# A minimum and a small product take their second operand as a scalar, and the attention stage is planned anew

## The chip, the cores and the metric

The kernel runs on one core of one Trainium2 chip. The metric is the device time of one launch in microseconds; the time before is a median of three runs. The engines are called TensorE (PE in the rows, PEld its weight loads), VectorE (DVE), ScalarE (ACT), GpSimd (POOL) and SyncE (SP, which issues the transfers).

## The reference, cut to what matters

One layer of a diffusion backbone: a normalised, modulated input projection feeds two groups of attention heads, then come an output projection and a SwiGLU feed-forward part. The change lies in attention. 1024 latent queries read 1024 latent keys and 256 context keys in one softmax:

```python
a = jax.nn.softmax(s1, axis=-1) - lam * jax.nn.softmax(s2, axis=-1)   # 4 heads, group A
a = jax.nn.softmax(s, axis=-1)                                        # 8 heads, group B
```

In group A each head has two score maps, s1 and s2, and the weighted difference of their softmaxes multiplies the values; in group B each head has one. Each softmax needs its row's maximum over all 1280 keys.

## The kernel before, in words

**Stages.** From 0 to about 324 us the kernel projects the input and writes queries, keys and values to HBM. From 324 to about 840 us it runs attention: two units of group B, then eight units of group A (4 heads by 2 halves of the queries), then the rest of group B. After that come the output projection and the feed-forward part.

**One block.** A unit of group A is four blocks of 128 queries. For a block TensorE writes two score maps of 1280 columns into one accumulator tile S of five banks: `latent` 0 and 1 fill 1024 columns each, `context` 256 columns of both maps in the bank between them (L1056). VectorE takes the negated maximum of the context columns of both maps in one instruction, `max_context` (nmc, L1068), and of the latent columns of each map, `max_latent` (nm, L1072). `least` (L1076) takes the smaller of the two, one number per partition; it is the bias of ScalarE's exponential `exp` (L1090), which also sums its row. S exists once, so the next block's `context` waits for both exponentials of this block.

**Between the maps.** In group A `factor` (L1097 a reciprocal, L1098 a product) makes -lam times the ratio of the two row sums, one number per partition. GpSimd then multiplies the second map by it (`weigh`, L1101) and adds the first (`combine`, L1104), both over 1280 columns. In group B GpSimd only divides by the row sum (`normalise`, L1110).

**Values.** For each of the ten 128-key chunks of a unit TensorE transposes four blocks (L1118), ScalarE copies the result as the high part (`high`, ph, L1122), VectorE subtracts it for the low part (`low`, pl, L1126), and TensorE multiplies both by the values (L1135, L1140).

**Order.** `attention_graph` lists all operations of the stage with an engine, an assumed duration, dependencies and a due number; `schedule` plays them as a list scheduler (of the operations ready on an engine the lowest due number goes first), and they are issued in the order of the planned starts. The due number is the block's or chunk's position plus an entry of the table PRIO, one entry per kind of operation. Each engine works through its own list strictly in order. The planned times do not depend on what the other engines do in the same moment.

The functions that the change touches, and what calls them:

Of the kernel before, what the change touches and what calls it, by code (L numbers as in the profile page):

```python
# [13 lines left out]
ALU = mybir.AluOpType  # L14
# [69 lines left out]
                put(user)  # L84


PRIO = {'up': 11.727086, 'mod': -18.756409, 'sum_mod': -32.213338, 'TA': 4.147972, 'TB': 8.034109, 'lagA': 0.698127, 'lagB': 0.960591, 'near': 0.126904, 'Alatent0': -26.812639, 'Acontext': -21.646222, 'Alatent1': 2.987414, 'Amax_latent0': -4.873014, 'Amax_context': -26.762829, 'Amax_latent1': -2.132328, 'Aexp0': -31.715337, 'Aexp1': 12.171988, 'Atranspose': 4.62933, 'Ahigh': 11.648332, 'Alow': 37.646643, 'Asum': 9.444701, 'Blatent0': 3.505773, 'Bcontext': 4.634551, 'Blatent1': 7.767885, 'Bmax_latent0': 2.818406, 'Bmax_context': -34.678605, 'Bmax_latent1': 7.503355, 'Bexp0': 30.917087, 'Bexp1': 13.50608, 'Btranspose': 0.882797, 'Bhigh': -25.097498, 'Blow': -2.25778, 'Bsum': 4.842969, 'factor': -19.46868, 'weigh': -21.351391, 'combine': -24.776362, 'inverse': 7.726575, 'normalise': -24.649633, 'square': 2.409828, 'diagonal': -2.156322, 'load': 0, 'out': 33.135816}


def attention_graph(prio=PRIO):  # L90

# [3 lines left out]
    def op(engine, time, deps, name, *args, kind=None, late=0.0):  # L95
        o = Op(engine, time, deps, base[0] + late + prio[kind or name], name, args)
        ops.append(o)
        return o
# [3 lines left out]
    def slot(tag, bufs):  # L102

        got = slots.setdefault(tag, [])
        return got[-bufs] if len(got) >= bufs else None

    x = [None, None]
    acc_free = None
    low_sum = []
# [4 lines left out]
    def after(tag, o):  # L114

        if tag in order:
            o.deps.append(order[tag])
        order[tag] = o
        return o

    def block(n, A):

        nonlocal x
        u, qh, b, j = n
        k = "A" if A else "B"
        w = 1.0 if A else 1.5
        need = [loads[u], loads[u, qh], loads.get((u, qh, j))]
        first = op("PE", 0.86 * w, need + [x[0]], "latent", n, 0, kind=k + "latent0")
        ctx_ = op("PE", 0.43 * w, need + x, "context", n, kind=k + "context")
        second = op("PE", 0.86 * w, need + [x[1]], "latent", n, 1, kind=k + "latent1")  # L130
        mc = op("DVE", 0.6, [ctx_], "max_context", n, kind=k + "max_context")
        m0 = op("DVE", 1.13, [first], "max_latent", n, 0, kind=k + "max_latent0")
        m1 = op("DVE", 1.13, [second], "max_latent", n, 1, kind=k + "max_latent1")
        l0 = op("DVE", 0.07, [m0, mc], "least", n, 0, kind=k + "max_latent0")
        l1 = op("DVE", 0.07, [m1, mc], "least", n, 1, kind=k + "max_latent1")
        tags = [("e1", 3) if A and b == 0 else ("e", 8), ("e2", 3) if A else ("e", 8)]
        x = []
        for i, l in enumerate((l0, l1)):
            x.append(after("exp", op("ACT", 1.3, [l, slot(*tags[i])], "exp", n, i, kind=k + f"exp{i}")))
            slots[tags[i][0]].append(None)  # L140
        for key in ((u, qh), (u, qh, j), ("kv", kvs[-1])):
            scored.setdefault(key, []).extend((first, second, ctx_))
        if A:
            f = op("DVE", 0.2, x, "factor", n)
            wt = op("Pool", 1.31, [f], "weigh", n)
            c = op("Pool", 2.84, [wt], "combine", n)
            slots["e2"][-1] = c
            return [c]
        done = []
        for i in range(2):  # L150
            f = op("DVE", 0.08, [x[i]], "inverse", n, i)
            done.append(op("Pool", 1.31, [f], "normalise", n, i))
        return done

    def chunk(c, ready, A):
        nonlocal acc_free
        k = "A" if A else "B"
        kc = c[3]
        t = after("T", op("PE", 0.436, ready + (T[-2] if len(T) > 1 else []), "transpose", c, kind=k + "transpose"))
        old = low_sum[-3:][:1] if len(low_sum) > 2 else []  # L160
        h = after("high", op("ACT", 0.478, [t] + old, "high", c, kind=k + "high"))
        l = after("low", op("DVE", 0.602, [h] + old, "low", c, kind=k + "low"))
        T.append([h, l])
        sh = op("PE", 0.43 if A else 0.215, [h, acc_free if kc == 0 else None] + low_sum[-1:], "sum_high", c, kind=k + "sum")
        low_sum.append(op("PE", 0.215, [l, sh], "sum_low", c, kind=k + "sum"))
        return t

    def finish(u, qh, j, A):
        nonlocal acc_free
        if A:  # L170
            acc_free = op("ACT", 0.478, low_sum[-1:] + low_done, "evac_a", u, qh, kind="Ahigh")
            evac[u, qh] = acc_free
        else:
            a = op("ACT", 0.478, low_sum[-1:] + (cats[-2] if j == 0 and len(cats) > 1 else []), "evac_b", u, qh, j, kind="Bhigh")
            acc_free = op("DVE", 0.602, [a], "add_b", u, qh, j, kind="Blow")
            if j == 0:
                cats.append([])
            if (u, qh) == (HA, 0):
                parked.append(((u, qh, j), acc_free))
            else:  # L180
                cat((u, qh, j), [acc_free], cats[-1])

    def cat(n, deps, to):
        h = op("ACT", 0.52, deps, "cat_high", *n, kind="Bhigh", late=5.0)
        to.extend([h, op("DVE", 0.6, [h], "cat_low", *n, kind="Blow", late=5.0)])

    cats, parked, kvs, qs, ropes = [], [], [], [], []

# [51 lines left out]
    low_done = []  # L240
    vt_last, t, root = {}, 0.0, None
    for i, (u, qh, j) in enumerate(units):
        A = u < HA
        per = prio["TA"] * 4 if A else prio["TB"] * 2
        base[0] = t
        if u != (units[i - 1][0] if i else None):
            kvs.append(i)
            old = kvs[-3:][:1] if len(kvs) > 2 else []
# [8 lines left out]
        for b in range(4 if A else 2):  # L257
            base[0] = t + b * (prio["TA"] if A else prio["TB"])
            ready += block((u, qh, b, j), A)
# [22 lines left out]
        for tag in ("e1", "e"):  # L282
            slots[tag] = [o or last for o in slots.get(tag, ())]
        vt_last[kvs[-1]] = low_sum[-1]
        finish(u, qh, j, A)
        if i == 2 * HA + 1:
            for n, o in parked:
                cat(n, [o, low_sum[-1]], cats[0])
# [7 lines left out]
    for d in range(FIRST + 1):  # L296
        f = op("DMA", 3.0, [before_last, fetched[d], summed if d > 1 else None], "fetch_out", d, kind="load")
        h = op("ACT", 0.95, [f], "high_out", d, kind="out")
# [7 lines left out]
def tile_hybrid_diffattn_mla_dit_layer(  # L306
# [18 lines left out]
    ACT, DVE, POOL, PE = nc.scalar, nc.vector, nc.gpsimd, nc.tensor  # L325
    dma = nc.sync.dma_start

    def pool(stack, name, side=None, space=None, bufs=1):
        kw = {}
        if side:  # L330
            kw["side"] = side
        if space is not None:
            kw["space"] = space
        if space is not DRAM:
            kw["reuse_waits"] = "tile"
        return stack.enter_context(tc.tile_pool(name=name, bufs=bufs, **kw))
# [35 lines left out]
    nlam = const.tile([P, 1], F32, name="nlam")  # L372
# [77 lines left out]
    x = sp.tile([P, KD, NT], F32, name="x")  # L450
# [135 lines left out]
    low = [(0, i) for i in range(3)] + [(1, i) for i in range(2)] + [(2, i) for i in range(2)]  # L586
# [121 lines left out]
    for j, (ps, (b, i)) in enumerate(zip(lows, low)):  # L708
        n = SLICES[i][1]
# [204 lines left out]
    for which, dst in ((0, KA), (1, QA)):  # L914
        for h in range(HA):
            next_weights()
            w = ahead.pop(0)
# [62 lines left out]
    class Attention:  # L980
# [92 lines left out]

        def least(self, n, i):
            nm, nmc = self.s[n][0][:, i:i + 1], self.s[n][1][:, i:i + 1]
            DVE.tensor_tensor(nm, nm, nmc, ALU.min)  # L1076

        def exp(self, n, i):
            u, qh, b, j = n
# [14 lines left out]
        def factor(self, n):  # L1094
            u, qh, b, j = n
            l1, l2 = l1st[:, u * 8 + qh * 4 + b:u * 8 + qh * 4 + b + 1], self.s[n][2][:, 1:2]
            DVE.reciprocal(l2, l2)  # L1097
            DVE.scalar_tensor_tensor(l2, l2, l1, nlam, ALU.mult, ALU.mult)  # L1098

        def weigh(self, n):  # L1100
            POOL.tensor_scalar(self.e[n, 1], self.e[n, 1], self.s[n][2][:, 1:2], 1.0, ALU.mult, ALU.mult)  # L1101
# [151 lines left out]
    ops = attention_graph()  # L1253
    schedule(ops, PRIO["near"])
    ops.sort(key=lambda o: o.start)
# [89 lines left out]
    op = pool(st, "outp", side="right")  # L1345
# [195 lines left out]
    with tc.manual_schedule(engines=ENGINES):  # L1541
        ws = [load_out(d) for d in range(KD - 2, KD)]
        for d in range(KD - 2, KD):
            ps = mm_tile()
            project(1, d, ps, ws.pop(0), range(8))
            if d == KD - 2:
                residual(1, d, ps)
                first = [Hidden(0, False), None]
# [64 lines left out]
    for j in range(2, NJ - 1):  # L1613
        h, ahead = ahead, Hidden(j + 1)
# [285 lines left out]
```

## Time and profile before

| what | value |
|---|---|
| time, median of 3 runs | 1641.59 us (1640.61 to 1644.83) |
| the profiled execution | 1640.7 us, its span 1638.9 us |
| TensorE busy over the span | 1519.1 us (93%) |
| VectorE busy | 1193.3 us (73%) |
| ScalarE busy | 759.6 us (46%) |
| GpSimd busy | 798.5 us (49%) |

Busy time is the time in which the engine has an instruction in work, including time in which an instruction that has begun is held up. Shares over the whole span hide that the stages have different limits, so the rows below go by stretches.

### The profile page before, as it was taken

Reading aid. Unit: us, or ns where it says so; the run is one execution under the profiler, and the core shown is the slowest. Engines: PE = TensorE matmul, PEld = TensorE weight load, DVE = VectorE, ACT = ScalarE, POOL = GpSimd, SP = SyncE. Lnnn points to the kernel's source line nnn. Section 1 sums busy time; section 2 is a strip of 40 time slices with the busy share of each in tenths; the row PEclk is TensorE's granted clock in tenths of the full one; section 3 lists DMA queues with packets and bytes.
Section 4 is the critical chain, followed back from the end, with each engine's and each line's share of the span. In section 5 each row is a group of like instructions: output and inputs, shape, how many; then the busy total and the mean of one; then the engine's idle time right before and its main releaser. Section 6 shows DMA issues by size and latency. Waiting matters only on the chain.

```text
span 1638.9 us, 20678 instructions
## 1 busy us (share of the span) xinstructions
PE 1519.1 (93%) x7323; PEld 1214.8 (74%) x7323; DVE 1193.3 (73%) x1642; ACT 759.6 (46%) x1192; POOL 798.5 (49%) x551
## 2 busy tenths in 40 slices
PE   4899999987778899999999989999999999999887
PEld 2577888765566678788877857888888888888766
DVE  5757565579999988999975588655555556869893
ACT  5443421265556557677764444333333333444251
POOL 2435335435656656755622275755544441437531
PEclk8999999999999999999999989999999999999997
DMA  8436987592332345453217412322222225963432
GB/s 252 138 96 223 319 280 226 186 265 87 84 90 72 71 97 142 110 157 82 65 52 212 154 45 71 110 90 84 77 84 78 77 78 185 369 235 136 159 116 103
DMA packets 153923, 227.70 MB, mean 139 GB/s; under 512 B 11215, under 2 KB 80859, under 8 KB 153819
## 3 DMA queue, kind: packets, MB, share of 16 engines
q1 hardware_dynamic: 153547, 226.11, 44.7%
q8 instruction: 58, 0.95, 0.2%
q14 instruction: 46, 0.38, 0.1%
q10 hardware_dynamic: 272, 0.26, 0.0%
HBM read 172.53 MB, written 53.81 MB: 138 GB/s over the span
## 4 chain that ended last, share of the span: by engine, by line
PE 58%; DVE 23%; DMA 6%; issue 4%; POOL 4%; ACT 3%; SPq 1%; DVEq 0%; ACTq 0%; POOLq 0%
PE mm L1427 24%; PE mm L1713 8%; PE S L1056 7%; DVE nm L1076 4%; PE T L1118 4%; DVE nm L1072 4%; PE mm L1355 3%; DVE pl L1126 3%; PE acc L1135 2%; DVE block L347 2%; PE acc L1140 2%; PE mm L410 2%; PE mm L600 1%; DVE nmc L1068 1%; PE ps L1355 1%
## 5 line engine op out<-in xcount | busy, mean ns | idle before, releaser
L1090 ACT ACTIVATE e<-S,nm 128x1280 f32<-128x1280 f32 x128 | 170.1, 1329 | 104.3 <-DVE nm L1076 79.9
L1056 PE MATMUL S<-kt,qt 128*128 128x512 f32 (+1 forms) x768 | 200.9, 370 | 13.6 <-ACT e L1090 11.4
L1713 PE MATMUL mm<-block 128*128 128x512 f32 x792 | 182.0, 392 | 6.8 <-DVE block L347 6.8
L1118 PE MATMUL T<-ident,e 128*128 128x128 f32 x960 | 147.8, 277 | 36.1 <-DVE pl L1126 32.1
L1713 PEld LDWEIGHTS mm<-block 128*128 128x128 f32 x792 | 149.5, 189 | 39.1 <-DVE block L347 8.1
L1122 ACT ACTIVATE ph<-T 128x512 fp32r<-128x512 f32 x240 | 142.1, 597 | 75.8 <-PE T L1118 71.7
L1118 PEld LDWEIGHTS T<-ident,e 128*128 128x128 f32 x960 | 115.1, 142 | 77.6 <-issue 29.9
L1126 DVE TENSOR_TENSOR pl<-T,ph 128x512 fp32r<-128x512 f32 x240 | 161.3, 682 | 15.0 <-ACT ph L1122 12.5
L1056 PEld LDWEIGHTS S<-kt,qt 128*128 128x128 f32 x768 | 132.2, 192 | 49.6 <-ACT e L1090 26.3
L1072 DVE TENSOR_REDUCE nm<-S 128x1 f32<-128x1024 f32 x128 | 155.8, 1217 | 15.6 <-PE S L1056 14.3
L1110 POOL TENSOR_SCALAR e<-e,ls 128x1280 f32<-128x1280 f32 x64 | 85.9, 1342 | 116.5 <-DVE ls L1107 101.0
L1135 PE MATMUL acc<-ph,vt 128*128 128x512 f32 x320 | 131.1, 450 | 2.0 <-ACT ph L1122 1.1
L1427 PE MATMUL mm<-fresh,wh 128*128 128x512 f32 x352 | 113.8, 402 | 3.3 <-DVE fresh L1580 2.9
L1427 PE MATMUL mm<-block,wh 128*128 128x512 f32 x352 | 112.3, 400 | 0.0
L1532 POOL TENSOR_TENSOR hd<-acc,v 128x512 f32<-128x512 f32 x22 | 29.6, 1344 | 147.3 <-DVE acc L1528 135.7
L344 ACT ACTIVATE wh<-wf 128x1024 fp32r<-128x1024 f32 (+1 forms) x51 | 52.2, 1026 | 103.6 <-issue 64.1
L1140 PE MATMUL acc<-pl,vt 128*128 128x512 f32 x240 | 99.3, 414 | 0.0
L1300 POOL TENSOR_TENSOR acc<-acc,sq 128x512 f32<-128x512 f32 x23 | 35.2, 1530 | 129.6 <-ACT sq L1298 129.0
L410 PE MATMUL mm<-hH,wh 128*128 128x512 f32 (+1 forms) x256 | 95.2, 372 | 0.0
L1104 POOL TENSOR_TENSOR e<-e,e 128x1280 f32<-128x1280 f32 x32 | 93.6, 2926 | 2.7
L410 PE MATMUL mm<-hH,wl 128*128 128x512 f32 (+1 forms) x256 | 93.9, 367 | 0.0
L410 PE MATMUL mm<-hL,wh 128*128 128x512 f32 (+1 forms) x256 | 93.8, 366 | 0.0
(367 smaller groups left out, 3705.5 us busy)
## 6 DMA issues: line engine op xcount, KB each, us to landing
wf<-in_w_ffn_in_dram SPq DMA_DIRECT2D x44, 512.0 KB, 3.8
hidD<-hd SPq DMA_DIRECT2D x44, 256.0 KB, 2.1
wh<-in_w_ffn_out_dram SPq DMA_DIRECT2D x21, 512.0 KB, 5.9
wl<-hidD SPq DMA_DIRECT2D x17, 512.0 KB, 6.5
wa<-in_w_ada_dram SPq DMA_DIRECT2D x16, 512.0 KB, 4.0
wa<-in_w_ada_dram SPq DMA_DIRECT2D x32, 256.0 KB, 3.7
qt<-QB SPq DMA_DIRECT2D x32, 256.0 KB, 4.4
qt<-QA SPq DMA_DIRECT2D x32, 256.0 KB, 4.9
```

The costliest lines, as they stand in the source:

```text
L410: PE.matmul(ps, a(k), b(k), start=start and i == 0, stop=stop and i == n - 1)
L1056: m = PE.matmul(S[:, c0:c0 + w], q, k[:, k0:k0 + w], start=s == 0, stop=s == len(job) - 1)
L1072: on_banks(DVE.tensor_reduce(self.stats(n)[0][:, i:i + 1], sl, AX.X, ALU.max, negate=True), BANKS[i], DVE)
L1090: m = ACT.activation(e, S[:, i * NT:(i + 1) * NT], AF.Exp, bias=self.s[n][0][:, i:i + 1], accum_out=total)
L1104: POOL.tensor_tensor(self.e[n, 0], self.e[n, 0], self.e[n, 1], ALU.add)
L1118: PE.transpose(self.T[c][:, b * P:(b + 1) * P], e[:, kc * P:(kc + 1) * P], ident)
L1122: ACT.activation(self.ph[c], self.T[c], AF.Copy)
L1126: DVE.tensor_tensor(self.pl[c], self.T[c], f32(self.ph[c]), ALU.subtract)
L1135: PE.matmul(self.acc[u, qh, j], vt[:, kc, v], self.ph[c], start=kc == 0 and i == 0, stop=False)
L1140: PE.matmul(self.acc[u, qh, j], self.kv[u][1][:, kc, v], self.pl[c], start=False, stop=kc == 9)
L1427: PE.matmul(ps, a[:, k, :], b, start=k == 0 and i == 0, stop=k == 3 and i == 2)
L1713: PE.matmul(ps[d], w[:, sl], x[:, t0:t0 + n], start=c == 0 and i == 0, stop=c == NH - 1 and i == 2)
```

## The change

It has three parts. `least` becomes a `tensor_scalar` instruction: nm is its one tensor, and nmc is a scalar operand read per partition. `factor`'s product becomes a `tensor_scalar` with two scalar operands (l1 and nlam) in place of a `scalar_tensor_tensor` with two tensors and one scalar. The reciprocals stay. The assumed durations in the graph and the table PRIO get new numbers, so the operations of the stage are issued in a new order; the operations themselves are the same.

```diff
         def least(self, n, i):
             nm, nmc = self.s[n][0][:, i:i + 1], self.s[n][1][:, i:i + 1]
-            DVE.tensor_tensor(nm, nm, nmc, ALU.min)
+            DVE.tensor_scalar(nm, nm, nmc, None, ALU.min)
...
             DVE.reciprocal(l2, l2)
-            DVE.scalar_tensor_tensor(l2, l2, l1, nlam, ALU.mult, ALU.mult)
+            DVE.tensor_scalar(l2, l2, l1, nlam, ALU.mult, ALU.mult)
```

Assumed durations (us), before and after: latent 0.86 and 0.93 (group B 1.5 times that), context 0.43 and 0.48, max_context 0.6 and 0.7, max_latent 1.13 and 1.23, least 0.07 and 0.2, exp 1.3 and 1.53, factor 0.2 and 0.4, weigh 1.31 and 1.35, combine 2.84 and 2.93, high 0.478 and 0.6, low 0.602 and 0.69, the two sums 0.43 and 0.215 becoming 0.46 and 0.231 in group A; a chunk's transposes stay at 0.436.

Of PRIO's entries these are spoken of below (before, after): Alatent0 -26.8, -30.3; Acontext -21.6, -13.9; Aexp0 -31.7, -17.8; Aexp1 12.2, 10.6; Ahigh 11.6, -1.3; Alow 37.6, 60.6; Atranspose 4.6, 2.8; Asum 9.4, 9.2.

## Rows read from the trace of the kernel before

**Rows 1.** Busy time per engine in five stretches; the first row names the columns.

```profile
core 0: us, PE busy (x) PEld busy (x) DVE busy (x) ACT busy (x) POOL busy (x), PEclk, DMA share, GB/s
324.00:600.00 276.00, 226.52 (x1174) 173.26 (x1174) 252.02 (x364) 161.76 (x253) 154.66 (x79) 0.98 0.46 118
600.00:840.00 240.00, 238.18 (x1390) 196.69 (x1389) 215.06 (x375) 175.56 (x281) 146.87 (x149) 1.00 0.38 103
840.00:1639.00 799.00, 765.15 (x3343) 619.27 (x3342) 528.54 (x599) 304.34 (x464) 358.30 (x217) 0.98 0.38 127
362.12:571.17 209.05, 166.25 (x857) 125.86 (x856) 197.66 (x275) 122.08 (x190) 124.13 (x61) 0.97 0.34 85
425.00:431.11 6.11, 6.10 (x35) 4.90 (x34) 5.93 (x13) 4.79 (x8) 4.65 (x3) 1.00 0.01 3
```

**Rows 2.** Chain of waits inside 324 to 600 us: share by line.

```profile
by line: DVE nm L1076 25.2%; DVE nm L1072 20.5%; DVE pl L1126 13.3%; PE S L1056 8.1%; DVE nmc L1068 6.9%; DMA QB<-stage 4.0%; ACT e L1090 3.8%; issue 3.3%; PE T L1118 3.1%; DVE ls L1098 2.2%; DMA qt<-QA 2.2%; DMA cn<-LOW 1.7%; PE acc L1135 
```

**Rows 3.** Waits inside 324 to 600 us: total, times, longest (us).

```profile
ACT e L1090 <- DVE nm L1076: 72.1, 45, 4.0
```

**Rows 4.** The stretches again, busy time of the minimum (L1076) alone.

```profile
324.00:600.00 276.00, 73.17 (x73) 0.98 0.46 118
...
362.12:571.17 209.05, 64.14 (x56) 0.97 0.34 85
```

**Rows 5.** One stretch, the context's maximum (L1068) alone.

```profile
362.12:571.17 209.05, 19.21 (x29) 0.97 0.34 85
```

**Rows 6.** Timeline, all engines: start, length (us), instruction, idle before.

```profile
409.50 2.94 POOL L1104 TENSOR_TENSOR e<-e,e 128x1280 f32<-128x1280 f32 x1
...
409.74 2.71 DVE L1076 TENSOR_TENSOR nm<-nm,nmc 128x1 f32<-128x1 f32 x1
...
412.55 1.33 ACT L1090 ACTIVATE e<-S,nm 128x1280 f32<-128x1280 f32 x1 [2.34 <-DVE nm L1076]
...
413.20 0.63 PE L1118 MATMUL T<-ident,e 128*128 128x128 f32 x4 [1.62 <-DVE pl L1126]
```

**Rows 7.** Timeline of one block from 425 us, VectorE, ScalarE, GpSimd.

```profile
425.00 0.69 DVE L1068 TENSOR_REDUCE nmc<-S 128x2 f32<-128x512 f32 x1 [1.38 <-PE S L1056]
...
425.93 0.15 DVE L1076 TENSOR_TENSOR nm<-nm,nmc 128x1 f32<-128x1 f32 x1
...
426.18 1.33 ACT L1090 ACTIVATE e<-S,nm 128x1280 f32<-128x1280 f32 x1 [1.84 <-PE T L1118]
...
427.50 0.59 ACT L1122 ACTIVATE ph<-T 128x512 fp32r<-128x512 f32 x1
427.61 2.96 POOL L1104 TENSOR_TENSOR e<-e,e 128x1280 f32<-128x1280 f32 x1
...
427.98 1.33 ACT L1090 ACTIVATE e<-S,nm 128x1280 f32<-128x1280 f32 x1
...
430.04 0.15 DVE L1097 RECIPROCAL ls<-ls 128x1 f32<-128x1 f32 x1
...
431.11 0.68 DVE L1068 TENSOR_REDUCE nmc<-S 128x2 f32<-128x512 f32 x1
```

**Rows 8.** Timeline, GpSimd and VectorE in the latent-head stage.

```profile
667.22 1.35 POOL L1110 TENSOR_SCALAR e<-e,ls 128x1280 f32<-128x1280 f32 x1 [0.54 <-DVE ls L1107]
...
667.75 0.74 DVE L1204 SCALAR_TENSOR_TENSOR oT<-oT,subln,T 128x512 f32<-128x512 f32 x1
```

**Rows 9.** Timeline, GpSimd and VectorE after attention.

```profile
950.09 2.41 POOL L347 TENSOR_TENSOR sl<-oT,sh 128x1024 fp32r<-128x1024 f32 x1 [1.50 <-ACT sh L344]
...
950.41 4.86 DVE L1316 TENSOR_SCALAR dg<-ident,rs 128x128 f32<-128x128 f32 x4
...
952.44 2.35 POOL L347 TENSOR_TENSOR wl<-oT,wh 128x1024 fp32r<-128x1024 f32 x1
```

**Rows 10.** Line L1098 alone: min/median/max of one, ns.

```profile
L1098 DVE SCALAR_TENSOR_TENSOR ls<-ls,l1st,nlam x32: 219/220/359, 361.4 to 591.9; 128x1 f32<-128x1 f32 x32
```

**Rows 11.** Line L1262 alone, the same columns.

```profile
L1262 DVE TENSOR_SCALAR nlam<-nlam x1: 155/155/155, 325.2 to 325.2; 128x1 f32<-128x1 f32 x1
```

More of the change, by code (lines that the diff above doesn't have):

```diff
@@ L84, in schedule @@
                 put(user)
-PRIO = {'up': 11.727086, 'mod': -18.756409, 'sum_mod': -32.213338, 'TA': 4.147972, 'TB': 8.034109, 'lagA': 0.698127, 'lagB': 0.960591, 'near': 0.126904, 'Alatent0': -26.812639, 'Acontext': -21.646222, 'Alatent1': 2.987414, 'Amax_latent0': -4.873014, 'Amax_context': -26.762829, 'Amax_latent1': -2.132328, 'Aexp0': -31.715337, 'Aexp1': 12.171988, 'Atranspose': 4.62933, 'Ahigh': 11.648332, 'Alow': 37.646643, 'Asum': 9.444701, 'Blatent0': 3.505773, 'Bcontext': 4.634551, 'Blatent1': 7.767885, 'Bmax_latent0': 2.818406, 'Bmax_context': -34.678605, 'Bmax_latent1': 7.503355, 'Bexp0': 30.917087, 'Bexp1': 13.50608, 'Btranspose': 0.882797, 'Bhigh': -25.097498, 'Blow': -2.25778, 'Bsum': 4.842969, 'factor': -19.46868, 'weigh': -21.351391, 'combine': -24.776362, 'inverse': 7.726575, 'normalise': -24.649633, 'square': 2.409828, 'diagonal': -2.156322, 'load': 0, 'out': 33.135816}
+PRIO = {'up': 9.7602, 'mod': -16.2433, 'sum_mod': -28.9039, 'TA': 4.3985, 'TB': 8.0341, 'lagA': 0.7749, 'lagB': 0.8936, 'near': 0.1269, 'Alatent0': -30.3466, 'Acontext': -13.9011, 'Alatent1': 7.0835, 'Amax_latent0': -5.541, 'Amax_context': -35.7654, 'Amax_latent1': -2.7267, 'Aexp0': -17.7871, 'Aexp1': 10.5797, 'Atranspose': 2.8018, 'Ahigh': -1.3379, 'Alow': 60.6189, 'Asum': 9.2393, 'Blatent0': 4.1956, 'Bcontext': 6.5453, 'Blatent1': 8.176, 'Bmax_latent0': 2.8184, 'Bmax_context': -35.8831, 'Bmax_latent1': 7.658, 'Bexp0': 32.9397, 'Bexp1': 14.8502, 'Btranspose': -4.6752, 'Bhigh': -25.4229, 'Blow': -2.2578, 'Bsum': 5.8057, 'factor': -30.7948, 'weigh': -14.4586, 'combine': -16.1753, 'inverse': 0.7428, 'normalise': -15.6487, 'square': -9.3928, 'diagonal': -2.1563, 'load': 0, 'out': 48.8141}
 def attention_graph(prio=PRIO):
@@ L127, in block @@
         need = [loads[u], loads[u, qh], loads.get((u, qh, j))]
[L128 to L135, printed above, removed]
+        first = op("PE", 0.93 * w, need + [x[0]], "latent", n, 0, kind=k + "latent0")
+        ctx_ = op("PE", 0.48 * w, need + x, "context", n, kind=k + "context")
+        second = op("PE", 0.93 * w, need + [x[1]], "latent", n, 1, kind=k + "latent1")
+        mc = op("DVE", 0.7, [ctx_], "max_context", n, kind=k + "max_context")
+        m0 = op("DVE", 1.23, [first], "max_latent", n, 0, kind=k + "max_latent0")
+        m1 = op("DVE", 1.23, [second], "max_latent", n, 1, kind=k + "max_latent1")
+        l0 = op("DVE", 0.2, [m0, mc], "least", n, 0, kind=k + "max_latent0")
+        l1 = op("DVE", 0.2, [m1, mc], "least", n, 1, kind=k + "max_latent1")
         tags = [("e1", 3) if A and b == 0 else ("e", 8), ("e2", 3) if A else ("e", 8)]
@@ L138, in block @@
         for i, l in enumerate((l0, l1)):
-            x.append(after("exp", op("ACT", 1.3, [l, slot(*tags[i])], "exp", n, i, kind=k + f"exp{i}")))
+            x.append(after("exp", op("ACT", 1.53, [l, slot(*tags[i])], "exp", n, i, kind=k + f"exp{i}")))
             slots[tags[i][0]].append(None)
@@ L143, in block @@
         if A:
-            f = op("DVE", 0.2, x, "factor", n)
-            wt = op("Pool", 1.31, [f], "weigh", n)
-            c = op("Pool", 2.84, [wt], "combine", n)
+            f = op("DVE", 0.4, x, "factor", n)
+            wt = op("Pool", 1.35, [f], "weigh", n)
+            c = op("Pool", 2.93, [wt], "combine", n)
             slots["e2"][-1] = c
@@ L150, in block @@
         for i in range(2):
-            f = op("DVE", 0.08, [x[i]], "inverse", n, i)
-            done.append(op("Pool", 1.31, [f], "normalise", n, i))
+            f = op("DVE", 0.16, [x[i]], "inverse", n, i)
+            done.append(op("Pool", 1.35, [f], "normalise", n, i))
         return done
@@ L160, in chunk @@
         old = low_sum[-3:][:1] if len(low_sum) > 2 else []
-        h = after("high", op("ACT", 0.478, [t] + old, "high", c, kind=k + "high"))
-        l = after("low", op("DVE", 0.602, [h] + old, "low", c, kind=k + "low"))
+        h = after("high", op("ACT", 0.6, [t] + old, "high", c, kind=k + "high"))
+        l = after("low", op("DVE", 0.69, [h] + old, "low", c, kind=k + "low"))
         T.append([h, l])
-        sh = op("PE", 0.43 if A else 0.215, [h, acc_free if kc == 0 else None] + low_sum[-1:], "sum_high", c, kind=k + "sum")
-        low_sum.append(op("PE", 0.215, [l, sh], "sum_low", c, kind=k + "sum"))
+        sh = op("PE", 0.46 if A else 0.231, [h, acc_free if kc == 0 else None] + low_sum[-1:], "sum_high", c, kind=k + "sum")
+        low_sum.append(op("PE", 0.231, [l, sh], "sum_low", c, kind=k + "sum"))
         return t
@@ L170, in finish @@
         if A:
-            acc_free = op("ACT", 0.478, low_sum[-1:] + low_done, "evac_a", u, qh, kind="Ahigh")
+            acc_free = op("ACT", 0.6, low_sum[-1:] + low_done, "evac_a", u, qh, kind="Ahigh")
             evac[u, qh] = acc_free
         else:
-            a = op("ACT", 0.478, low_sum[-1:] + (cats[-2] if j == 0 and len(cats) > 1 else []), "evac_b", u, qh, j, kind="Bhigh")
-            acc_free = op("DVE", 0.602, [a], "add_b", u, qh, j, kind="Blow")
+            a = op("ACT", 0.6, low_sum[-1:] + (cats[-2] if j == 0 and len(cats) > 1 else []), "evac_b", u, qh, j, kind="Bhigh")
+            acc_free = op("DVE", 0.69, [a], "add_b", u, qh, j, kind="Blow")
             if j == 0:
@@ L183, in cat @@
     def cat(n, deps, to):
-        h = op("ACT", 0.52, deps, "cat_high", *n, kind="Bhigh", late=5.0)
-        to.extend([h, op("DVE", 0.6, [h], "cat_low", *n, kind="Blow", late=5.0)])
+        h = op("ACT", 0.62, deps, "cat_high", *n, kind="Bhigh", late=5.0)
+        to.extend([h, op("DVE", 0.9, [h], "cat_low", *n, kind="Blow", late=5.0)])
     cats, parked, kvs, qs, ropes = [], [], [], [], []
```

## The prediction, before the changed kernel was run

> **What bounds the kernel now.** I read the stretches first. From 600 to 840 us TensorE is busy 238.18 of 240.00 us: what the change does to VectorE there is hidden behind TensorE. After 840 us no minimum is left, and those 799.00 us stay. From 324 to 600 us, the stage of group A, it is the other way round: VectorE is busy 252.02 of 276.00 us, TensorE 226.52 [rows 1]. The chain of waits inside that stage then names the instruction: 25.2% of it is L1076, the minimum of two single columns [rows 2], and ScalarE's exponentials stood 72.1 us waiting for it [rows 3]. 73 of them took 73.17 us there [rows 4], 1.0 us each, while one that nothing disturbs takes 0.15 us [rows 7]. The timeline shows what disturbs them. At 409.50 us GpSimd began a `combine` of 2.94 us, ending at 412.44; the minimum began at 409.74 and ended 2.71 us later, at 412.45; the exponential, idle for 2.34 us, began at 412.55, and TensorE's next transposes had waited 1.62 us for a `low` queued behind the minimum [rows 6]. So a minimum that meets a GpSimd instruction is held to its end, and VectorE's queue with it.
>
> **The hold, priced.** Over the price of an undisturbed minimum the stage pays 73.17 - 73 x 0.15 = 62.2 us. For the rate I take the 28 blocks between the first and the last of 29 `max_context` [rows 5]: 209.05 us, 7.47 us a block, in which 56 minima took 64.14 us [rows 4]; 64.14 - 56 x 0.15 = 55.7 us are hold, 2.0 us a block.
>
> **The minimum as `tensor_scalar`.** Two questions: is it still held, and what does it cost when free? For the first, rows point both ways. A two-tensor minimum reads two SBUF columns and is held. A `scalar_tensor_tensor` with one SBUF tensor, an SBUF scalar and a PSUM tensor is not: at 667.75 us one ran 0.74 us inside a GpSimd instruction from 667.22 to 668.57 [rows 8], the length it has in all 8 of its line, each of which overlaps a GpSimd instruction. A one-column reciprocal at 430.04 us took 0.15 us inside a `combine` of 427.61 to 430.57 [rows 7]. Against that stands a row with the very operation: four `tensor_scalar` of 128 columns, with a scalar per partition, took 4.86 us beside two GpSimd instructions and were still in work when the second ended, at 954.79 [rows 9]. I side with the first two, because with a single column these are nearest in size, and since a scalar operand alone held nothing up. That the other case holds is a rival below.
>
> [...]
>
> For the second question: the one-column `tensor_scalar` with a constant took 155 ns [rows 11], the one-column product with a scalar per partition 219 to 220 ns undisturbed [rows 10]. I take 0.22, nearest in operands; the other end is 0.155. Then 73 minima cost 16.1 us where they cost 73.17: **57.1 us** off VectorE in the stage. In the 28 blocks it is 64.14 - 56 x 0.22 = 51.8 us.
>
> **`factor`.** The product is 220 ns before [rows 10] and by the same nearest row 220 after. Its longest was 359 ns, so over 32 it can give back at most 32 x 0.14 = 4.5 us, and far less since its median is 220; a second scalar read could cost, by the gap between 155 and 220, 0.065 x 32 = 2.1 us. I take zero.
>
> **What is late next.** If all of it came off the path, 28 blocks would take 209.05 - 51.8 = 157.3 us, 5.62 a block. Two things stand near that. TensorE: a block in which both minima were almost undisturbed, from 425.00 to 431.11 us, ran 35 matmuls in 6.11 us at 6.10 us busy [rows 1], 0.174 us each. The 28 blocks have 857, so 149.4 us, 5.34 a block: TensorE doesn't stop it before 5.62, but VectorE (197.66 - 51.8 = 145.9 us) and TensorE would be over 92% full together. And the ring through the single S: maximum of the context 0.69, minimum, exponential 1.33, exponential 1.33, next context, next maximum. Free of holds it took 6.11 us in that block, and a `high` of 0.59 stood between the two exponentials [rows 7]. The ring decides in such a block and the VectorE sum in a lighter one, so I take 5.95, between 5.62 and 6.11 and nearer the measured one. That saves 28 x (7.47 - 5.95) = 42.6 us of the possible 51.8, 82%; the rest of the stage holds 57.1 - 51.8 = 5.3 us, at the same share 4.3. Together **46.9 us**.
>
> **The new order.** No operation is added or dropped, the loads keep their due entry of 0 and follow the heads that they serve; a faster group A brings them closer together, with the transfer engines at 0.46 in the stage [rows 1], so I count nothing for them. What its order is worth no row shows. Below: TensorE's 5.34 a block, 28 x 0.61 = 17 us beyond the forecast at the very most, and I count 8 of these. Above: context is due later against the transposes than before (-13.9 and 2.8, before -21.6 and 4.6), and Ahigh at -1.3 now goes ahead of Aexp1 at 10.6 wherever both are ready, where they were level. A `high` of 0.59 more in every ring makes 6.54 a block and takes 28 x 0.59 = 16.5 us back. I take zero, between the two. From 600 to 840 us the order can't gain, as TensorE is 99% full.
>
> **The sum.** The profiled execution took 1640.7 us: 1640.7 - 46.9 = 1593.8. It lies 0.9 us under the median, so 1594.7 against the median; I say **1595**. Within this case: all of it off the path, 1641.6 - 57.1 = 1584.5; 6.4 a block, 28 x 1.07 = 30.0 plus 5.3 x 30.0/51.8 = 3.1, so 1608.
>
> **Rivals.**
>
> *The ring becomes the bound.* A further `high` in each ring: 6.54 a block, 28 x 0.93 = 26.0 and 2.7 for the rest, 1613. For it: S exists once and the ring of the free block was 6.11 already; Ahigh's number. Against: the free block's 6.11 us held 35 matmuls, more than the mean of 30.6, and such a `high` already.
>
> *The minimum is still held.* The change then doesn't do what it says: holds stay and each undisturbed minimum costs 0.07 more, 73 x 0.07 = 5 us at most, so 1642 to 1646, say 1644. For it the 128-column rows; against it the one-column reciprocal and the scalar operand that held nothing.
>
> *The order lengthens the ring past what the hold gave.* Slower. The place is between two contexts in group A: a `high` (0.59) ahead of the second exponential and a `low` (0.68) ahead of the next maximum, and TensorE's transposes and sums ahead of the next context. It decides from 7.47 - 5.95 = 1.52 us of such queueing per block, two to three instructions; at 2.0 us a block it costs 28 x 0.48 = 13 us, 1655. For it only the numbers of Acontext and Ahigh; against it that due numbers decide only between operations that are ready together in the plan.
>
> *The order also closes the gaps.* TensorE near 5.4 a block: 1641.6 - 57.1 - 4 = 1580.
>
> **How the numbers follow.** Forecast 0.70, ring as bound 0.16, tighter order 0.05, still held 0.05, slower order 0.04. The range goes from 1581, the tighter order's edge, to 1619, a few microseconds past the ring case, and leaves out the last two cases and the tails. About 0.3%, 5 us, is what a measurement of this kernel tells from no change: faster 0.92, within 0.04 (most of the still-held case), slower 0.04.
>
> **What would show it.** Right: L1076 as one `tensor_scalar` of about 0.22 us at minimum, median and maximum, also where a `combine` runs; VectorE's busy time from 324 us to the end of group A down by some 57 us and TensorE's share there above 90%; blocks of about 6.0 us; ScalarE's wait for nm down from 72.1 us to under 20; group A ending near 553 us in place of 600. Wrong: minima of 1 to 3 us ending with a GpSimd instruction (still held), or free minima with ScalarE and TensorE waiting in turn for the context (the ring), or a loss from 600 us on, which I have put at nothing.

## The result, and the profile after

The changed kernel takes 1589.54 us in the median of 4 runs (1588.49 to 1591.05), against 1641.1 us for the kernel before beside it: 0.9693 of its time, with an interval of 0.9671 to 0.9715. The profiled execution spans 1588.6 us, before 1638.9.

The stretches of the kernel after, in the columns of [rows 1]: the stage of group A, the rest of attention, 28 blocks of group A between two `max_context`, the start of the output projection, and all that follows.

```profile
core 0: us, PE busy (x) PEld busy (x) DVE busy (x) ACT busy (x) POOL busy (x), PEclk, DMA share, GB/s
324.00:551.00 227.00, 214.89 (x1192) 173.80 (x1193) 201.72 (x371) 164.73 (x258) 156.99 (x81) 1.00 0.55 144
551.00:786.00 235.00, 233.07 (x1371) 195.05 (x1370) 208.51 (x369) 170.17 (x276) 145.84 (x148) 1.00 0.39 105
362.85:525.33 162.48, 154.96 (x868) 124.44 (x867) 150.40 (x276) 122.48 (x192) 125.25 (x62) 1.00 0.44 109
802.70:851.70 49.00, 47.31 (x196) 37.45 (x195) 23.28 (x28) 20.23 (x28) 9.32 (x6) 0.97 0.64 187
851.70:1588.60 736.90, 706.68 (x3060) 574.43 (x3058) 496.36 (x557) 275.01 (x422) 345.26 (x211) 0.97 0.37 125
```

To be read against [rows 1]: the same 28 blocks took 209.05 us and take 162.48, 5.80 a block in place of 7.47. TensorE was busy 166.25 of 209.05 us there, 80%, and is busy 154.96 of 162.48, 95%. The granted clock (PEclk, the clock that TensorE was given, as a share of full speed) was 0.97 in those blocks and is 1.00; before, it was 0.50 in four stretches of 3.4 us, beginning at 396.9, 420.8, 451.5 and 482.2 us, and TensorE was idle for 43 us of those blocks. After attention the granted clock is lower than before in these two executions. The two rows of the kernel before that answer to the last two, first the start of the output projection:

```profile
856.20:903.30 47.10, 45.40 (x196) 36.26 (x194) 22.24 (x28) 20.22 (x29) 9.13 (x6) 1.00 0.66 194
903.30:1638.90 735.60, 703.72 (x3060) 570.88 (x3058) 495.94 (x557) 275.71 (x422) 349.17 (x211) 0.98 0.37 125
```

47.10 became 49.00 us at a granted clock of 0.97 in place of 1.00, and 735.60 became 736.90 us: 3.2 us longer where nothing was changed. That this comes from the change is not shown. From the start of the last `normalise` to the end it is 800.8 us before and 804.5 after, but two kernels of the experiments below that do the same work there in the same order, the old order with the scalar operands and the one-line version, take 799.5 and 804.4.

The chain of waits of the kernel after inside 324 to 551 us, share by line:

```profile
by line: PE S L1056 29.3%; PE T L1118 15.5%; PE acc L1135 9.6%; POOL e L1104 6.5%; PE acc L1140 5.3%; ACT e L1090 4.1%; DVE nm L1072 3.2%; DMA QB<-stage 3.2%; POOL e L1101 3.0%; DVE nmc L1068 2.7%; issue 2.7%; DMA qt<-QA 2.7%; DMA cn<-LOW 2
```

The minimum, 25.2% of the chain in [rows 2], is not among the lines that the row shows; TensorE's scores lead with 29.3%. Two waits of that stretch (total, times, longest). The first answers to [rows 3]; in the second the weight loads of the next scores wait for the exponentials to free S:

```profile
ACT e L1090 <- DVE nm L1076: 29.3, 29, 2.9
...
PEld S L1056 <- ACT e L1090: 13.6, 19, 2.0
```

The first wait, 72.1 us before, is 29.3 us. The minimum's line, all 128 of it, with min/median/max in ns:

```profile
L1076 DVE TENSOR_SCALAR nm<-nm,nmc x128: 194/214/218, 328.3 to 781.5; 128x1 f32<-128x1 f32 x128
```

None is above 218 ns. One of them in the timeline, inside a `combine` that runs from 468.81 to 471.76 us, where the one of [rows 6] took 2.71 us:

```profile
468.81 2.95 POOL L1104 TENSOR_TENSOR e<-e,e 128x1280 f32<-128x1280 f32 x1
...
470.42 0.21 DVE L1076 TENSOR_SCALAR nm<-nm,nmc 128x1 f32<-128x1 f32 x1
```

All instances tell the same. Before, 74 of the 128 minima began inside a GpSimd instruction; none of them ended more than 0.03 us ahead of it, and all 51 minima longer than 0.3 us ended within 0.03 us of the end of a GpSimd instruction. In the changed kernel 80 begin inside one, and 64 of these end more than 0.03 us ahead of it. So the minima have not been moved out of GpSimd's way; they no longer wait.

And the product of `factor`, 219/220/359 before [rows 10]:

```profile
L1098 DVE TENSOR_SCALAR ls<-ls,l1st,nlam x32: 272/273/276, 362.6 to 542.9; 128x1 f32<-128x1 f32 x32
```

### The profile page after: what moved, and what is told of

Same layout as the page of the kernel before. It is cut to its first block, busy times and chain, and to the rows that moved or that the text cites. A ratio compares the mean times of both kernels' runs of the same rounds, so it can differ in the third digit from the quotient of the medians.

```text
span 1588.6 us, 20701 instructions
## 1 busy us (share of the span) xinstructions
PE 1508.9 (95%) x7323; PEld 1221.4 (77%) x7323; DVE 1137.5 (72%) x1642; ACT 756.3 (48%) x1192; POOL 793.2 (50%) x551
## 4 chain that ended last, share of the span: by engine, by line
PE 69%; DVE 12%; DMA 6%; POOL 4%; issue 3%; ACT 3%; SPq 1%; POOLq 0%; ACTq 0%; DVEq 0%
PE mm L1427 25%; PE S L1056 10%; PE mm L1713 8%; PE T L1118 6%; PE acc L1135 4%; PE mm L1355 3%; PE acc L1140 3%; DVE block L347 2%; PE mm L410 2%; PE mm L600 2%; PE ps L1355 1%; PE S L1355 1%; DMA wa<-in_w_ada_dram 1%; POOL sh L645 1%; POOL e L1104 1%
## 5 line engine op out<-in xcount | busy, mean ns | idle before, releaser
L1118 PE MATMUL T<-ident,e 128*128 128x128 f32 x960 | 140.4, 274 | 3.0 <-DVE pl L1126 1.7
L1135 PE MATMUL acc<-ph,vt 128*128 128x512 f32 x320 | 120.9, 418 | 1.1 <-DVE otmp L1156 1.0
L1140 PE MATMUL acc<-pl,vt 128*128 128x512 f32 x240 | 104.6, 436 | 0.0
L1104 POOL TENSOR_TENSOR e<-e,e 128x1280 f32<-128x1280 f32 x32 | 94.2, 2943 | 2.7
```

The source lines that it names most:

```text
L1104: POOL.tensor_tensor(self.e[n, 0], self.e[n, 0], self.e[n, 1], ALU.add)
L1118: PE.transpose(self.T[c][:, b * P:(b + 1) * P], e[:, kc * P:(kc + 1) * P], ident)
L1135: PE.matmul(self.acc[u, qh, j], vt[:, kc, v], self.ph[c], start=kc == 0 and i == 0, stop=False)
L1140: PE.matmul(self.acc[u, qh, j], self.kv[u][1][:, kc, v], self.pl[c], start=False, stop=kc == 9)
```

## The experiments

Two theories stood at the start. *Hold*: the gain is the hold that the minimum no longer meets, and the order is worth little. *Order*: the new plan made the gain, or a part of it, by moving things apart. Three further questions followed: why a `tensor_scalar` escapes, what bounds group A now, and where the two orders differ.

**The old order with the scalar operands.** Only the two instructions are changed in the kernel before:

```diff
-            DVE.tensor_tensor(nm, nm, nmc, ALU.min)
+            DVE.tensor_scalar(nm, nm, nmc, None, ALU.min)
...
-            DVE.scalar_tensor_tensor(l2, l2, l1, nlam, ALU.mult, ALU.mult)
+            DVE.tensor_scalar(l2, l2, l1, nlam, ALU.mult, ALU.mult)
```

> The two scalar-operand instructions in the order of before (its assumed durations and its due numbers). If the hold by GpSimd is what went, the minima here take about 0.21 us each as in the changed kernel, the stage of group A loses most of its 57 us of hold, and the time is 1590 to 1602 us; what is missing to 1589.5 is what the order is worth. If the new order made the gain, the time stays above 1620 us.

Measured: 1584.03 us, 0.9657 (0.9641 to 0.9673) of before. It is 5.5 us less than the changed kernel. Its 28 blocks:

```profile
360.54:517.53 156.99, 152.25 (x857) 122.92 (x856) 147.22 (x274) 121.79 (x190) 124.54 (x61) 1.00 0.46 114
```

156.99 us, 5.61 a block. So the hold explains the whole gain, and the new order takes some of it back, which neither theory had. The intervals of the two ratios just touch (0.9671 to 0.9673); what makes the loss clear is that the four runs here, 1579.79 to 1584.44 us, all lie under the four of the changed kernel, 1588.49 to 1591.05, and that the new order measured beside it, with the old product (below), has 0.9693 to 0.9722.

**The new order with two tensors.** The changed kernel with both old instructions:

```diff
-            DVE.tensor_scalar(nm, nm, nmc, None, ALU.min)
+            DVE.tensor_tensor(nm, nm, nmc, ALU.min)
...
-            DVE.tensor_scalar(l2, l2, l1, nlam, ALU.mult, ALU.mult)
+            DVE.scalar_tensor_tensor(l2, l2, l1, nlam, ALU.mult, ALU.mult)
```

> The new order with the two-tensor minimum and the two-tensor product. If the hold is the cause, minima of 1 to 3 us that end with a GpSimd instruction are back and the time is 1632 to 1646 us. If the order made the gain, by taking the minima out of the stretches in which GpSimd works, the minima's mean stays under 0.4 us and the time is below 1605 us.

Measured: 1635.33 us, 0.9984 (0.9962 to 1.0007): no change that can be told. The minimum's line:

```profile
L1076 DVE TENSOR_TENSOR nm<-nm,nmc x128: 137/230/2678, 330.3 to 829.2; 128x1 f32<-128x1 f32 x128
```

The holds are back, up to 2.68 us. By itself the order is worth nothing measurable.

**Two columns in place of one.** The same operation and scalar, one element more. The input column is read twice, the two equal results go to a small tile of their own, and the exponential reads the first of them:

```diff
-            DVE.tensor_scalar(nm, nm, nmc, None, ALU.min)
+            two = self.s[n][3][:, 2 * i:2 * i + 2]
+            DVE.tensor_scalar(two, nm.to_broadcast([P, 2]), nmc, None, ALU.min)
```

> The changed kernel, but the minimum writes two equal columns (its one input column read twice), so that its free size is 2 in place of 1; the exponential reads the first. [...] If a scalar operand in place of a second tensor is what frees it, the minima stay near 0.21 us and the time is 1589 to 1592 us.

Measured: 1639.69 us, 0.9988 (0.9971 to 1.0006). The line (L1078 in this kernel), then one of it in the timeline with the `combine` (here L1106) and the exponential (L1092):

```profile
L1078 DVE TENSOR_SCALAR two<-nm,nmc x128: 207/247/2700, 326.6 to 838.9; 128x2 f32<-128x2 f32 x128
```

```profile
422.27 2.94 POOL L1106 TENSOR_TENSOR e<-e,e 128x1280 f32<-128x1280 f32 x1
...
423.36 1.87 DVE L1078 TENSOR_SCALAR two<-nm,nmc 128x2 f32<-128x2 f32 x1
...
425.33 1.33 ACT L1092 ACTIVATE e<-S,two 128x1280 f32<-128x1280 f32 x1 [1.12 <-DVE two L1078]
```

The two-column minimum began at 423.36 us, in a `combine` that ends at 425.21, and ended at 425.23. Of all 128 none is over more than 0.03 us ahead of a GpSimd instruction in which it began. The whole gain is gone. So it isn't the scalar operand as such that frees this minimum, but the scalar operand together with a single column: one column with two tensors took up to 2678 ns (above), two columns with a scalar up to 2700, one column with a scalar at most 218.

**The old product.** The changed kernel with the two-tensor product alone put back:

```diff
-            DVE.tensor_scalar(l2, l2, l1, nlam, ALU.mult, ALU.mult)
+            DVE.scalar_tensor_tensor(l2, l2, l1, nlam, ALU.mult, ALU.mult)
```

> The changed kernel with the old two-tensor product in factor; the minimum stays as changed. The product took 273 ns as changed and 220 ns before, so 32 of them give 1.7 us back to VectorE unless they are held; if the product's form doesn't matter the time is 1588 to 1592 us. If products are held by GpSimd as the minima were (up to 2.9 us each, in a good part of the 32), weigh and combine come later and the time is 1594 to 1605 us.

Measured: 1591.84 us, 0.9708 (0.9693 to 0.9722), not to be told from the changed kernel. Its line:

```profile
L1098 DVE SCALAR_TENSOR_TENSOR ls<-ls,l1st,nlam x32: 219/220/993, 362.5 to 545.4; 128x1 f32<-128x1 f32 x32
```

220 ns in the median, but five of the 32 took over 300 ns, up to 993, and each of the five ended with a GpSimd instruction. So this product can be held too; 11 of the 32 began inside a GpSimd instruction. All 32 together take 10.9 us in place of 8.7, which doesn't show in the time.

**Old due numbers with new durations, and the reverse.** The first is the changed kernel with the old PRIO, the second the old order's kernel above with the new PRIO. (The new durations also contain some of group B that the list of the change leaves out, as `inverse` 0.16 in place of 0.08.)

```diff
-PRIO = {'up': 9.7602, 'mod': -16.2433,
...
+PRIO = {'up': 11.727086, 'mod': -18.756409,
...
```

> The changed kernel (scalar operands, new assumed durations) with the old table of due numbers. The old order as a whole gave 1584 us with the scalar operands, the new one 1589.5. If the new due numbers cost the difference, this gives 1582 to 1586 us; if the new assumed durations do, 1588 to 1592 us; if only the two together suit each other, it is above 1592 us.

```diff
-PRIO = {'up': 11.727086, 'mod': -18.756409,
...
+PRIO = {'up': 9.7602, 'mod': -16.2433,
...
```

> The scalar operands and the new due numbers with the old assumed durations. If the new assumed durations cost the 5.5 us between the two orders, this gives 1582 to 1586 us; if the due numbers do, 1588 to 1592 us; if each table was fitted to its own durations, above 1592 us.

Measured: 1596.57 us, 0.9724 (0.9703 to 0.9745), and 1598.16 us, 0.9730 (0.9710 to 0.9750). All eight runs are slower than every run of the changed kernel, though the intervals of the ratios overlap or touch. Where the time goes, the first and last starts of `combine` and `normalise` tell, for the changed kernel, the old order, and these two in the order above:

```profile
L1104 POOL TENSOR_TENSOR e<-e,e x32: 2924/2944/2957, 364.5 to 544.7; 128x1280 f32<-128x1280 f32 x32
L1110 POOL TENSOR_SCALAR e<-e,ls x64: 1326/1342/2362, 330.3 to 784.1; 128x1280 f32<-128x1280 f32 x64
```

```profile
L1104 POOL TENSOR_TENSOR e<-e,e x32: 2925/2948/2963, 361.6 to 535.5; 128x1280 f32<-128x1280 f32 x32
L1110 POOL TENSOR_SCALAR e<-e,ls x64: 1331/1337/2405, 328.7 to 778.4; 128x1280 f32<-128x1280 f32 x64
```

```profile
L1104 POOL TENSOR_TENSOR e<-e,e x32: 2921/2944/2962, 363.4 to 545.5; 128x1280 f32<-128x1280 f32 x32
L1110 POOL TENSOR_SCALAR e<-e,ls x64: 1325/1340/2172, 328.0 to 792.2; 128x1280 f32<-128x1280 f32 x64
```

```profile
L1104 POOL TENSOR_TENSOR e<-e,e x32: 2921/2944/2957, 363.9 to 545.4; 128x1280 f32<-128x1280 f32 x32
L1110 POOL TENSOR_SCALAR e<-e,ls x64: 1328/1340/1364, 328.9 to 794.8; 128x1280 f32<-128x1280 f32 x64
```

From the first `combine` to the last, group A's part, it is 180.2 us in the changed kernel, 173.9 in the old order, and 182.1 and 181.5 in the mixed ones: there either half of the replanning alone loses as much as both. From the last `combine` to the last `normalise`, the rest of group B, it is 239.4, 242.9, 246.7 and 249.4: there the whole new plan gains 3.5 us on the old one, and either half alone loses. That each table was fitted to its own durations would explain the second part; no run shows it.

**The context earlier.** In the changed kernel's plan, and in group A alone, each `context` is issued up to two transposes or sums earlier on TensorE:

```diff
     ops.sort(key=lambda o: o.start)
+    for o in [o for o in ops if o.name == "context" and o.args[0][0] < HA]:
+        for _ in range(2):
+            at_ = ops.index(o)
+            prev = max(i for i, p in enumerate(ops[:at_]) if p.engine == "PE")
+            if ops[prev].name not in ("transpose", "sum_high", "sum_low") or prev < max(ops.index(d) for d in o.deps):
+                break
+            ops.insert(prev, ops.pop(at_))
```

> The changed kernel, but in group A each context is issued up to two TensorE operations (transposes, sums) earlier, not ahead of where its second exponential is issued. In the changed kernel the context began 0.59 us after the second exponential's end on the mean, in the old order with scalar operands 0.30 us, and TensorE stands 0.78 us waiting for an exponential once in four blocks. If that ring is where the new order loses its 5.5 us, that wait shrinks and the time is 1583 to 1588 us. If TensorE's own work is the bound, nothing is won and the early contexts make TensorE wait: 1589 to 1596 us.

Measured: 1591.07 us, 0.9690 (0.9675 to 0.9705). Its 28 blocks:

```profile
360.85:526.84 165.99, 156.65 (x868) 125.15 (x866) 150.56 (x277) 121.59 (x190) 124.84 (x61) 1.00 0.44 106
```

165.99 us, longer than the 162.48 it was meant to shorten. The edit did move the contexts: by the trace, a context began 0.17 us after the end of the second exponential in the mean of the 28 blocks, where it is 0.60 in the changed kernel and 0.29 in the old order. But from there to its maximum it took 1.00 us in place of 0.77, and from the first exponential's start to the second's 2.20 in place of 2.01. A context that comes too late behind transposes is not, by itself, what the new order loses.

**One line.** The kernel before with the minimum changed and nothing else:

```diff
-            DVE.tensor_tensor(nm, nm, nmc, ALU.min)
+            DVE.tensor_scalar(nm, nm, nmc, None, ALU.min)
```

> The kernel before with one line changed: the minimum by a scalar operand; the product stays with two tensors, and the order stays. If the hold of the minimum is the whole cause, this gives 1582 to 1587 us, level with the old order with both lines (1584.0) and under the changed kernel (1589.5); the product's form is worth at most 1.7 us (53 ns less for each of 32). If products are held often in this order, 1588 us or more.

Measured over 5 rounds: 1579.97 us, 0.9628 (0.9607 to 0.9649). Its 28 blocks:

```profile
361.61:518.38 156.77, 152.24 (x857) 123.02 (x856) 146.93 (x274) 121.60 (x190) 124.59 (x61) 1.00 0.46 114
```

156.77 us, as with both lines. This one-line version is faster than both kernels: its interval lies below the changed kernel's 0.9671 to 0.9715. From the old order with both lines (0.9641 to 0.9673) it can't be told.

**What bounds group A now.** Three kernels take work from the changed one; the third makes both of these edits.

```diff
             u, qh, j, kc = c
+            if u < HA and kc < 9:
+                return
             v = slice(j * P, (j + 1) * P) if u >= HA else slice(0, P)
             PE.matmul(self.acc[u, qh, j], self.kv[u][1][:, kc, v], self.pl[c], start=False, stop=kc == 9)
```

> The changed kernel, leaving out in group A nine of every ten products of the low part with the values: 72 matmuls of some 0.23 us, 16.7 us less for TensorE; the order of the rest is as it was. If TensorE's work is now the bound of group A (155.0 of 162.5 us busy in 28 blocks), 10 to 16 us go: 1573 to 1580 us. If VectorE's queue or the ring through S is, 0 to 5 us go: 1585 to 1590 us.

```diff
-            sl = S[:, i * (NT + 256):i * (NT + 256) + NL]
+            sl = S[:, i * (NT + 256):i * (NT + 256) + (NL if n[0] >= HA else NL // 2)]
```

> The changed kernel with the latent maxima of group A taken over 512 of the 1024 columns: 64 instructions some 0.53 us shorter, 34 us less for VectorE. If VectorE's queue is the bound of group A (150.4 of 162.5 us busy), 10 to 20 us go until TensorE's 5.4 us a block stops it: 1576 to 1582 us. If TensorE's work is, 0 to 4 us go: 1586 to 1590 us.

> Both of these together. If the ring through S (5.0 us of fixed pieces and latencies a block, by the trace of the changed kernel) is what holds the stage once neither engine is full, the blocks stay at 5.3 us or more and the time is above 1575 us. If the two engines were the bounds, blocks fall under 5.2 us and the time lies at 1565 to 1573 us.

Measured: 1584.43, 1586.45 and 1578.29 us; 0.9651 (0.9622 to 0.9680), 0.9651 (0.9623 to 0.9680) and 0.9614 (0.9588 to 0.9639). The same 28 blocks of each, in this order:

```profile
361.03:523.28 162.25, 150.10 (x814) 115.76 (x813) 149.95 (x276) 121.27 (x192) 125.33 (x62) 0.98 0.44 109
```

```profile
363.86:522.64 158.78, 152.27 (x868) 125.08 (x867) 123.08 (x276) 120.99 (x192) 125.01 (x62) 1.00 0.45 110
```

```profile
363.19:520.21 157.02, 146.62 (x814) 117.13 (x813) 122.56 (x275) 120.33 (x192) 125.13 (x62) 0.98 0.46 112
```

Against 162.48 us they take 162.25, 158.78 and 157.02. With fewer matmuls the blocks don't get shorter; with VectorE busy 27 us less they get 3.7 us shorter; with both relieved a block still takes 5.61 us. So neither engine's sum of work alone bounds group A, although TensorE is 95% busy there. TensorE's busy time fell by only 4.9 us for 54 fewer matmuls, some 12 us by the 0.23 us each that was expected (an estimate), so its 95% hold slack; and with fewer products the granted clock was 0.98, which by 2% of 150 us may hide 3 us of what was won, again an estimate.

That what is left is the order of events round the single S is argued from this and not shown: no run shortens that ring itself, and GpSimd, whose `weigh` and `combine` are 16.5% of the chain of waits in the 28 blocks with both relieved, was not relieved. The old order, too, reaches 5.61 us a block with all of the work in place. One block of the changed kernel shows how the ring can make TensorE wait (ScalarE and TensorE):

```profile
482.07 1.33 ACT L1090 ACTIVATE e<-S,nm 128x1280 f32<-128x1280 f32 x1
...
482.85 0.60 PE L1118 MATMUL T<-ident,e 128*128 128x128 f32 x4
...
483.20 0.48 PE L1140 MATMUL acc<-pl,vt 128*128 128x512 f32 x1
...
483.52 0.60 PE L1118 MATMUL T<-ident,e 128*128 128x128 f32 x4
...
483.87 1.65 PE L1056 MATMUL S<-kt,qt 128*128 128x256 f32 x8
...
485.98 1.33 ACT L1090 ACTIVATE e<-S,nm 128x1280 f32<-128x1280 f32 x1 [1.23 <-DVE nm L1076]
...
487.38 1.33 ACT L1090 ACTIVATE e<-S,nm 128x1280 f32<-128x1280 f32 x1
...
487.45 1.20 PE L1056 MATMUL S<-kt,qt 128*128 128x512 f32 x4 [0.78 <-ACT e L1090]
```

The second exponential ended at 483.40; the context followed at 483.87 behind a chunk's transposes; the next exponentials ran at 485.98 and 487.38; and TensorE, with the following block's scores next in its list, waited 0.78 us for the first of them to free its half of S. Such waits are 4.7 us of the 28 blocks, in 6 places.

## Why the prediction was right, point by point

The time, 1589.5 us, lies inside the range and within the forecast case's own 1584 to 1608; the direction and the mechanism were right. That it came within 6 us of the 1595 is in part luck. In the old order the same hold gave 1584.03 us, and 1579.97 with one line; I let too little of it through, and the loss by the new order, which I took at nothing, made up for a part of that.

*The hold.* Right. The 73 minima of the stage that took 73.17 us [rows 4] are 74 that take about 0.21 us each, none held. My price of 0.22 for the free one was close (0.214 in the median).

*That a one-column `tensor_scalar` escapes.* Right, and now shown from both sides: of the 80 one-column minima that began inside a GpSimd instruction 64 ended more than 0.03 us ahead of it, and none took over 218 ns; of the two-column ones none ended that far ahead, and they took up to 2700 ns. Of my two grounds, the single column is borne out; a scalar operand alone is not enough, as the two columns had one as well. Why the second column matters is not shown.

*The path.* I let 82% of the 51.8 us through in the 28 blocks, at 5.95 us a block; measured 46.6 us, 90%, at 5.80. The mis-sized term is this share: I took the block near the 6.11 us of the one free block, as the length of the ring, and in the old order nothing was lost at all (209.05 - 156.99 = 52.1 us, one for one). The `high` between that block's exponentials was not the reason for its length: 16 of the 28 blocks of the old order have one too, at 5.61 us a block. What that block had more of is time from the end of its second exponential, 429.31 us, to the next `max_context`: 1.80 us, where the mean is now 1.37, and 1.23 in the old order. It held 35 matmuls with TensorE busy 6.10 of 6.11 us [rows 1], so it points to TensorE's work and not to a ring free of it. That the ring and not the engines would be the next limit is not shown: 5.61 us a block remained with both relieved, but what holds the blocks there stays open.

*`factor`.* I took zero; each product costs 53 ns more (273 against 220), 1.7 us in all, within the 2.1 that I gave as the end. It doesn't show in the time.

*The new order.* I took zero between 8 us gained and 16.5 lost. With two-tensor minima that is what it is worth; with scalar operands it costs about 5.5 us in the medians. The profiled executions show a loss of 5.5 us in the 28 blocks (162.48 against 156.99), 6.3 from the first `combine` to the last, and a gain of 3.5 in the rest of attention. Of my two reasons for a loss, Ahigh is out: 15 of the 28 blocks have a `high` between their exponentials, 16 in the old order. Contexts do begin later, by 0.31 us a block, but pulling them forward won nothing. Which pieces of the order lose the time stays open; what the profiles show is that it is lost in group A's blocks, and that with held minima the same order shows no loss.

*What I put at nothing.* After attention the profiled execution is 3.2 us longer than before, 1.9 of them in 49 us of the output projection, in which the granted clock fell to 0.97. I had counted those 799 us as unchanged, and no run shows otherwise: executions with the same work there differ by 4.9 us.

*The signs.* The minimum's line and TensorE's 95% came as described. Blocks of 5.80 us came for about 6.0, and group A's last `combine` began 49.0 us earlier than before and ended at 547.7 us, where I had named 553. VectorE's busy time in the stage fell from 252.02 to 201.72 us, 50.3 where I had named some 57, with seven instructions more in the shorter stretch. ScalarE's wait for nm stayed at 29.3 us where I had named under 20: no minimum is held any more, and what the rest of this wait consists of was not taken apart.

The rivals: the still-held minimum is out by the minimum's line, the slower order by the time. The ring as bound forecast 1613 us by one more `high` in each ring, and that did not come. The tighter order is out as well: the new order lost time in group A.

## What to carry to other kernels

An instruction that handles 128 numbers in 0.15 us can be a quarter of a stage's critical chain (25.2% here, [rows 2]): look at the spread of its durations, and at which other engine's instruction ends where it ends. When an instruction's form is changed and the plan of the stage redone in one step, time the form alone too: here one line gave more than the whole change, and the redone plan gave part of it back. An engine at 95% busy need not be the bound (with 54 matmuls fewer for TensorE the 28 blocks took 162.25 us, with all of them 162.48); take work from it and see whether the stage moves.

## What the runs showed of the hardware that was not expected

For the minimum with a scalar operand, the step from one column to two decides: the `tensor_scalar` of one column took at most 218 ns in 128 instances, the same with two columns took up to 2700 ns, and 94.2 us for the 128 of its line (mean 736 ns) where the one-column line takes some 27. And in the one-line version the granted clock of the 28 blocks is 1.00, where it was 0.97 before [rows 1], without any change to TensorE's work; TensorE was idle for 43 us of these blocks before and is idle for 4.5 now. That the idle time set the clock is not shown.
